# 128 unused bytes in SBUF, and two families of tiles 4128 instead of 4096 bytes apart

## The chip, the cores and the metric

The kernel runs on one core of one Trainium2 chip. The metric is the device time of one execution in microseconds. Three runs of the kernel before took 797.56, 796.80 and 796.42 us: a median of 796.8 us.

## The reference

Two layers of a decoder trunk run over one sequence of 256 tokens with 1024 features each, all in float32:

```
for l in range(2):
    h = rms_norm(x, attn_norm[l])
    x = x + hybrid_mixer(h, ...)     # three token mixers side by side: MLA, MoBA, retention
    h = rms_norm(x, mlp_norm[l])
    x = x + square(relu(h @ w_mlp_up[l])) @ w_mlp_down[l]      # 1024 -> 4096 -> 1024
return rms_norm(x, final_norm)

def hybrid_mixer(h, w_in, ...):
    p = h @ w_in                                               # 1024 -> 6560
    o_mla, o_moba, o_ret = ...                                 # three attentions over slices of p
    merged = (sigmoid(g_mla) * (o_mla @ w_branch_mla)
              + sigmoid(g_moba) * (o_moba @ w_branch_moba)
              + sigmoid(g_ret) * (o_ret @ w_branch_ret))
    return merged @ w_out
```

Nearly all arithmetic is in the weight products: 1024 to 6560, three of 512 to 1024, 1024 to 1024, 1024 to 4096 and back.

## The kernel before, in words

**Products in three parts.** Each float32 matrix is cut into a high part (float32r, the format that TensorE streams) and the low rest, and each product is made of three matmuls: high by high, high by low, low by high. The helper `three` (lines 301 to 304) writes them: line 302 is high times `whi`, line 303 high times `wlo`, line 304 the low part times `whi`. In most of them the activations are the stationary operand, a block of 128 by 128 that TensorE loads ahead of the matmul, and the weights are the moving operand, 512 columns that stream through it.

**Weights.** They come in tiles of 128 partitions by 1024 elements (4096 bytes per partition) from one DRAM tensor, in the order in which they are used. `high_low` (lines 268 to 282) casts each into `whi` on ScalarE (line 274) and takes the rest `wlo` on VectorE (line 276). These tiles lie in a pool of their own, which the change does not touch.

**Activations.** The pool `sb` holds the rest. In it a *tag* is a ring of equally large buffers, each of the size of the largest tile that uses the tag, one behind the other in SBUF; the order of the tags is that of their first use. Two rings matter here:

- `t4`, nine buffers: the normed inputs `xs0` to `xs3` (each holds high and low part of two blocks of 128 features), the attention outputs `omlah`, `omlal`, `omobah`, `omobal`, `oreth`, `oretl`, the turned low-rank inputs `cTh`, `cTl`, the squared relus `relu` before they are turned, and some raw weights at the start (`raw0`).
- `w4k`, seven buffers: the turned relus `hidden`, high and low part in a tile each, the gates `th`, and other results of 1024 elements.

Behind them lie the ring of small tiles, the scratch tiles of the rope (`ropea`, `ropeb`), and then `Q`, `KK`, `blocks`, `prob` and `turned`. Some operands of matmuls borrow buffers there: `sums` (combinations of normed inputs for the seven-product scheme of the first MLP product) lies in those of `KK` and `prob`, and `mT` (the merged mixers, the moving operand of the output product at line 1099) in those of `Q` and `KK`.

**Order.** The program is written unit by unit (`prog`, `run`), and a scheduler orders the instructions within what the dependences allow; some stretches of TensorE are written out by hand. Waits are semaphores between the engines; transfers are issued by SyncE.

Of the kernel before, what the change touches and what calls it, by code (L numbers as in the profile page):

```python
# [7 lines left out]
F32 = mybir.dt.float32  # L8
# [5 lines left out]
P = 128  # L14
# [177 lines left out]
def trunk(ctx: ExitStack, tc: tile.TileContext, gx, wts, consts, gfin, gnorm, xtok, out):  # L192
# [7 lines left out]
    sb = ctx.enter_context(tc.tile_pool(name="sb", bufs=1))  # L200
# [20 lines left out]
    nc.gpsimd.memset(sq_cols, 0.0)  # L221
    nc.gpsimd.memset(sq_in, 0.0)
    krx = [cp.tile([P, P], F32, name=f"krx{t}") for t in range(NT)]
    for t in range(NT):
        nc.gpsimd.memset(krx[t], 0.0)

# [10 lines left out]
    started, high_first, middle = {}, [], []  # L237

    def transfer(key, raw, queue=nc.sync, parts=1):
        offset, n, c = where[key]  # L240
        sz = n * c
        for cs in (slice(0, sz),) if parts == 1 else (slice(0, 416), slice(416, sz)):
            queue.dma_start(
                raw[:, cs],
                bass.AP(tensor=wts.tensor, offset=wts.offset + offset + cs.start, ap=[[sz, P], [1, cs.stop - cs.start]]),
            )
# [42 lines left out]
        return sb.tile([P, 512], F32, name=name, tag="w2k", bufs=W2K)  # L289

    def w4k(name, dtype=F32):
        return sb.tile([P, 1024], dtype, name=name, tag="w4k", bufs=W4K)

    def two(name):
        both = w4k(name)
        return [both[:, :512], both[:, 512:]]
# [4 lines left out]
    def three(o, ah, al, bh, bl, start, stop, shared=False):  # L301
        nc.tensor.matmul(o, ah, bh, start=start, stop=False, skip_group_check=shared)  # L302
        nc.tensor.matmul(o, ah, bl, start=False, stop=False, skip_group_check=shared)  # L303
        nc.tensor.matmul(o, al, bh, start=False, stop=stop, skip_group_check=shared)  # L304
# [154 lines left out]
    def rope(xv, c0, s0, t, n, h, w=None):  # L459

        w = w or n
        cos = K[:, c0 + t * w : c0 + t * w + n][:, None, None, :].to_broadcast([P, h, 2, n])
        sin = K[:, s0 + t * w : s0 + t * w + n][:, None, None, :].to_broadcast([P, h, 2, n])
        a = sb.tile([P, 256], F32, name="ropea", bufs=1)
        b = sb.tile([P, 256], F32, name="ropeb", bufs=1)
        av = a[:, : 2 * h * n].rearrange("p (h two n) -> p h two n", h=h, two=2)
        bv = b[:, : 2 * h * n].rearrange("p (h two n) -> p h two n", h=h, two=2)
        nc.vector.tensor_mul(av, xv, cos)
        nc.vector.tensor_mul(bv, xv, sin)
        nc.vector.tensor_sub(xv[:, :, 0, :], av[:, :, 0, :], bv[:, :, 1, :])  # L470
        nc.vector.tensor_add(xv[:, :, 1, :], av[:, :, 1, :], bv[:, :, 0, :])
# [154 lines left out]

    def begin(key, tag=None, bufs=None, queue=nc.sync, parts=1):
        if tag:
            started[key] = sb.tile([P, 512 if tag == "w2k" else 1024], F32, name="raw0", tag=tag, bufs=bufs)
        else:  # L630
            started[key] = wp.tile([P, 1024], F32, name="raw", bufs=RAW)
        transfer(key, started[key], queue, parts)

    nc.sync.dma_start(GX[:, : G_END + S], gx[:, : G_END + S])
    begin((0, "b0", 0), "w2k", W2K, nc.scalar)
    begin((0, "mq", 0), "w2k", W2K)
    nc.scalar.dma_start(X[0][:, 1, :], x[:, 1, :])
    xn = Normed(G_ATT)
    xrows = [x for _ in range(NT) for x in two("xrow")]
    begin((0, "b0mq", 1), "t4", T4, parts=2)  # L640
    nc.sync.dma_start(X[0][:, 2:4, :], x[:, 2:4, :])
    begin((0, "b0mq", 2), "t4", T4)
# [14 lines left out]
    one = nc.const_aps.tensor(1.0, [P, 1], mybir.dt.bfloat16)  # L657
    for i in range(WARM):
        nc.tensor.matmul(pw, one.to_broadcast([P, P]), one.to_broadcast([P, 512]), start=True, stop=True)
# [17 lines left out]
    def layer(l, xn, before):  # L677
# [6 lines left out]
        def c_norms():  # L684
            accs = b0
            if l:
                for n in range(KD):
                    xn.square(n)
                xn.stats()
            c0.extend(two("c0"))  # L690
            for t, ct in enumerate(c0):
                nc.scalar.activation(ct[:, :416], accs[t][:, :416], AF.Copy, scale=xn.col[t])
                m = small("ssc")
                junk = sb.tile([P, S], F32, name="junk", tag="xsq", bufs=2)
                nc.scalar.activation(junk, ct[:, 0:MLA_QR], AF.Square, accum_out=m[:, 0:1])
                nc.scalar.activation(junk[:, :MLA_KVR], ct[:, MLA_QR : MLA_QR + MLA_KVR], AF.Square, accum_out=m[:, 1:2])
                nc.vector.tensor_scalar(m[:, 2:3], m[:, 0:1], 1.0 / MLA_QR, EPS, op0=ALU.mult, op1=ALU.add)
                nc.vector.tensor_scalar(m[:, 3:4], m[:, 1:2], 1.0 / MLA_KVR, EPS, op0=ALU.mult, op1=ALU.add)
                nc.gpsimd.tensor_tensor(m[:, 4:6], m[:, 2:4], neghalf[:, 0:2], op=ALU.pow)
                nc.vector.tensor_scalar(ct[:, 0:MLA_QR], ct[:, 0:MLA_QR], m[:, 4:5], None, op0=ALU.mult)  # L700
                kv = ct[:, MLA_QR : MLA_QR + MLA_KVR]
                nc.vector.tensor_scalar(kv, kv, m[:, 5:6], None, op0=ALU.mult)
                kr = ct[:, 384:416].rearrange("p (h two n) -> p h two n", h=1, two=2)
                rope(kr, K_COS_MLA, K_SIN_MLA, t, 16, 1, 32)
                for i in range(2):
                    dst = krx[t][:, 64 * (1 - i) : 64 * (1 - i) + 64].rearrange("p (two n) -> p two n", two=2)
                    nc.vector.tensor_copy(dst[:, :, 16 * i : 16 * i + 16], kr[:, 0, :, :])
# [100 lines left out]
        def qrope():  # L808
            wh, wl = load_w(l, "qrope", 0)
            qr = mla["qr"] = halves(w2k("qr"))  # L810
            for t in range(NT):
                acc = misc_tile()
                sl = slice(P * t, P * t + P)
                for k in range(2):
                    three(acc[:, :S], c["h"][:, k, sl], c["l"][:, k, sl], wh[:, k, :], wl[:, k, :], k == 0, k == 1)
                nc.scalar.activation(qr[:, t, :], acc[:, :S], AF.Copy)
                rope(qr[:, t, :].rearrange("p (h two n) -> p h two n", h=4, two=2), K_COS_MLA, K_SIN_MLA, t, 32, 4)
# [334 lines left out]
        def prepare(kind, i):  # L1152

            def load(c):
                return [load_w(l, "up", 4 * i + c + j) for j in range(2)]

            def parts(raw):
                return [high_low((l, "up", i), x, 2, 1024) for x in raw]

            b = blocks.setdefault(i, {})  # L1160
            if kind == "up":
                return load_w(l, "up", i)
            if kind == "down":
                return load_w(l, "down", i, 0)
            if kind == "m1":
                b["a"], b["c"] = load(4), load(0)
            elif kind in ("n3", "m2"):
                b[kind] = load(2 if kind == "n3" else 6)
            w = parts(b[{"n3": "n3", "m2": "m2", "n7": "c"}.get(kind, "a")])
            if kind == "m1":  # L1170
                add_tiles(b["a"], b["c"])
            elif kind == "n3":
                add_tiles(b["c"], b["n3"])
                add_tiles(b["a"], b["n3"])
            elif kind == "m2":
                add_tiles(b["a"], b["m2"])
            return w
# [81 lines left out]
        def down(w, t, half, f):  # L1259

            cs, (hi, lo) = slice(512 * half, 512 * half + 512), hidden[f][t]
            three(accs[2 * t + half], hi, lo, w[0][:, 0, cs], w[1][:, 0, cs], f == 0, f == NF - 1)
# [44 lines left out]
        for event, i, kind, j in mlp_events(l):  # L1307
            if event == "prepare":
                prepared[i] = prepare(kind, j)
                continue  # L1310
            if i == len(units) - ENDS:
                break
# [38 lines left out]
        if last:  # L1351
            gf = sb.tile([P, 2, D], F32, name="gf", tag="KK", bufs=1)
            nc.sync.dma_start(gf[:, 0, :], bass.AP(tensor=gfin.tensor, offset=gfin.offset, ap=[[0, P], [1, D]]))
        ws = [prepared.pop(i) if i in prepared else prepare(*units[i]) for i in range(len(units) - ENDS, len(units))]
        order_pe = ExitStack()
        order_pe.enter_context(tc.manual_schedule(engines={mybir.EngineType.PE}))

        def finish(q, fs):
            for i in fs:
                down(ws[i], *quarters[q], NF - ENDS + i)  # L1360

# [50 lines left out]
        for t in range(NT):  # L1412
# [12 lines left out]
            else:  # L1425

                more = misc_tile("plast")
                for half, o in enumerate((accs[3], more)):
                    cs = slice(512 + 256 * half, 768 + 256 * half)
                    for i, w in enumerate(ws):  # L1430
                        three(
                            o[:, 0:256], *hidden[NF - ENDS + i][1], w[0][:, 0, cs], w[1][:, 0, cs],
                            half == 1 and i == 0, i == ENDS - 1,
                        )
# [40 lines left out]
W4K = 7  # L1475
# [7 lines left out]
XIN = (36, 39, 42, 45)  # L1483
XSQ = (44, 46, 49, 50, 53)
WARM = 8
ENDS = 4
FIRST = 4
AHEAD = 1
# [79 lines left out]
```

## Time and profile before

| What | Value |
|---|---|
| Median of three runs | 796.8 us |
| The profiled execution: its time | 797.22 us |
| Its span, from the first to the last instruction | 795.3 us |
| TensorE matmuls: busy | 788.0 us (99% of the span), 3780 records |
| VectorE busy | 671.6 us (84%) |
| ScalarE busy | 527.6 us (66%) |
| Mean granted TensorE clock | 0.999 |
| Matmuls on the chain that ended last | 98% of the span |

How to read it: a matmul's duration in the trace goes from its start to the last of its results, and the next one starts before that. So durations of neighbouring matmuls overlap, and what one costs in a row is the time from its start to the next start. Groups are named by line, engine, operation, and output <- inputs; the last numbers of a group are its busy time, the mean duration of one in ns, and the idle time of the engine before them.

### The profile page before, as it was taken

The numbers are of one execution on the slowest core, as the hardware profiler recorded it, in microseconds if no ns is written. First come the engines' busy times: TensorE is split into PE (matmuls) and PEld (weight loads), VectorE is DVE, ScalarE is ACT, GpSimd is POOL, SyncE is SP. The second block draws the span as 40 slices with busy tenths as digits, with TensorE's granted clock in tenths as the row PEclk, the third lists the DMA queues.
The fourth block names the chain that finished last, engine by engine and source line by source line (L and its number), as shares of the span: only waits on it lengthen the run. The fifth ranks groups of instructions, "written<-read, shape, count | busy, mean of one in ns | idle before, by whom it ended". The sixth has DMA issues, their size and how long they took to land.

```text
span 795.3 us, 11143 instructions
## 1 busy us (share of the span) xinstructions
PE 788.0 (99%) x3780; PEld 654.0 (82%) x3780; DVE 671.6 (84%) x1121; ACT 527.6 (66%) x821; POOL 22.0 (3%) x36
## 2 busy tenths in 40 slices
PE   9999999999999999999999999999999999999996
PEld 7888878888888888888888888788888888888885
DVE  6887897687799999998589578968878999999984
ACT  7786656544577877777586767546455778676772
POOL 0100000100000000003100000001000000000000
PEclk9999999999999999999999999999999999999999
DMA  9895989587564997667567678895975559888771
GB/s 351 306 323 187 297 271 296 204 269 247 172 238 133 278 303 255 222 198 253 190 209 250 219 229 266 296 308 175 297 248 169 191 164 324 268 283 254 256 239 54
DMA packets 76105, 192.76 MB, mean 242 GB/s; under 512 B 8576, under 2 KB 32784, under 8 KB 76048
## 3 DMA queue, kind: packets, MB, share of 16 engines
q1 hardware_dynamic: 75312, 191.20, 73.6%
q10 hardware_dynamic: 576, 0.83, 0.3%
q8 instruction: 30, 0.49, 0.2%
q14 instruction: 27, 0.22, 0.1%
q0 software_dynamic: 160, 0.02, 0.0%
HBM read 169.97 MB, written 22.04 MB: 241 GB/s over the span
## 4 chain that ended last, share of the span: by engine, by line
PE 98%; DVE 1%; DMA 0%; ACT 0%; issue 0%; POOL 0%; POOLq 0%
PE acc L302 23%; PE acc L304 22%; PE acc L303 22%; PE acc L1099 6%; PE pup L303 5%; PE pup L302 5%; PE pup L304 5%; PE po L577 1%; PE ps_s L863 1%; PE ps_s L545 1%; PE misc L303 1%; PE misc L304 1%; PE misc L302 1%; PE acc L751 0%; PE acc L754 0%; PE acc L752 0%
## 5 line engine op out<-in xcount | busy, mean ns | idle before, releaser
L274 ACT ACTIVATE whi<-raw 128x1024 fp32r<-128x1024 f32 (+3 forms) x261 | 263.9, 1026 | 145.5 <-PE acc L304 77.5
L276 DVE TENSOR_TENSOR wlo<-raw,whi 128x1024 fp32r<-128x1024 f32 (+3 forms) x262 | 303.3, 1173 | 48.7 <-ACT whi L274 48.1
L302 PE MATMUL acc<-whi,xs 128*128 128x512 f32 (+1 forms) x448 | 175.1, 394 | 0.0
L303 PE MATMUL acc<-wlo,xs 128*128 128x512 f32 (+1 forms) x448 | 174.4, 389 | 0.0
L304 PE MATMUL acc<-whi,xs 128*128 128x512 f32 (+1 forms) x448 | 173.9, 389 | 0.0
L302 PEld LDWEIGHTS acc<-whi,xs 128*128 128x128 f32 x448 | 84.1, 188 | 18.0 <-issue 1.7
L304 PEld LDWEIGHTS acc<-whi,xs 128*128 128x128 f32 x448 | 84.1, 188 | 17.1
L303 PEld LDWEIGHTS acc<-wlo,xs 128*128 128x128 f32 x448 | 84.2, 188 | 16.6
L303 PE MATMUL acc<-wlo,hidden 128*128 128x512 f32 (+1 forms) x256 | 97.1, 388 | 0.0
L304 PE MATMUL acc<-whi,hidden 128*128 128x512 f32 (+1 forms) x256 | 93.7, 389 | 0.0
L302 PE MATMUL acc<-whi,hidden 128*128 128x512 f32 (+1 forms) x256 | 83.9, 389 | 0.0
L274 ACT ACTIVATE whi<-rawlong 128x1024 fp32r<-128x1024 f32 x60 | 62.7, 1055 | 17.3 <-DVE rawlong L1181 8.7
L276 DVE TENSOR_TENSOR wlo<-rawlong,whi 128x1024 fp32r<-128x1024 f32 x60 | 71.9, 1218 | 1.7 <-ACT whi L274 1.6
L304 PEld LDWEIGHTS acc<-whi,hidden 128*128 128x128 f32 x256 | 48.1, 188 | 10.5 <-DVE hidden L322 0.4
L303 PEld LDWEIGHTS acc<-wlo,hidden 128*128 128x128 f32 x256 | 48.1, 188 | 10.1
L302 PEld LDWEIGHTS acc<-whi,hidden 128*128 128x128 f32 x256 | 48.1, 188 | 9.9
L1181 DVE TENSOR_TENSOR rawlong<-rawlong,raw 128x1024 f32<-128x1024 f32 x36 | 43.5, 1211 | 1.2 <-DMA raw<-wts 1.2
L529 ACT ACTIVATE prob<-prob,smx 128x128 f32<-128x128 f32 x64 | 28.3, 443 | 15.8 <-DVE smx L525 15.8
L303 PE MATMUL pup<-wlo,sums 128*128 128x512 f32 x96 | 38.0, 396 | 0.0
L304 PE MATMUL pup<-whi,sums 128*128 128x512 f32 x96 | 37.9, 395 | 0.0
L302 PE MATMUL pup<-whi,sums 128*128 128x512 f32 x96 | 37.3, 395 | 0.0
L1099 PE MATMUL acc<-mT,whi 128*128 128x512 f32 x128 | 33.6, 396 | 0.0
(279 smaller groups left out, 1156.2 us busy)
## 6 DMA issues: line engine op xcount, KB each, us to landing
raw<-wts SPq DMA_DIRECT2D x240, 512.0 KB, 4.9
blocks<-far SPq DMA_DIRECT2D x104, 128.0 KB, 3.8
rawlong<-wts SPq DMA_DIRECT2D x24, 512.0 KB, 5.8
far<-relu SPq DMA_DIRECT2D x16, 512.0 KB, 4.6
far<-blocks SPq DMA_DIRECT2D x16, 384.0 KB, 4.1
turned<-far SPq DMA_DIRECT2D x64, 96.0 KB, 3.5
raw<-wts SPq DMA_DIRECT2D x6, 464.0 KB, 7.6
raw<-wts SPq DMA_DIRECT2D x4, 416.0 KB, 5.6
```

The lines of the kernel that those rows point to most:

```text
L274: nc.scalar.activation(hi[:, cs], raw[:, cs], AF.Copy)
L276: nc.vector.tensor_sub(lo[:, cs], raw[:, cs], hi[:, cs].bitcast(F32))
L302: nc.tensor.matmul(o, ah, bh, start=start, stop=False, skip_group_check=shared)
L303: nc.tensor.matmul(o, ah, bl, start=False, stop=False, skip_group_check=shared)
L304: nc.tensor.matmul(o, al, bh, start=False, stop=stop, skip_group_check=shared)
L529: nc.scalar.activation(p[:, j, a:b], p[:, j, a:b], AF.Exp, bias=m[:, 4 + c : 5 + c], scale=scale, accum_out=m[:, 8 + c : 9 + c])
L545: nc.tensor.matmul(o, a[rows], b[rows], start=True, stop=True)
L577: nc.tensor.matmul(dst, vh, moving, start=i == 0, stop=i == 1)
L863: nc.tensor.matmul(o[:, P : 3 * P], q[:, P:S], k, start=True, stop=True)
L1099: nc.tensor.matmul(o, w_k, m, start=wide and k == 0, stop=(k, wide) == jobs[-1] and k == KD - 1)
L1181: nc.vector.tensor_add(x, x, y)
```

## The change

Two numbers in the allocation of SBUF change, and no instruction is added or removed. Each engine of the two built programs has the same instructions in the same order, operand for operand except for the addresses.

1. `w4k` allocates 1024 + STEP elements, STEP being 8, and hands out the first 1024. So the seven buffers are 4128 bytes apart in place of 4096. The same is done to the raw weights that `begin` puts into the ring `t4` at the start, and since they are now the largest tiles of that ring, its nine buffers are 4128 bytes apart too.
2. The first call of `rope` allocates a tile `pad` of 32 elements (128 bytes) that nothing reads or writes.

The buffers then start at these bytes modulo 256, as the two programs place them (the built address of each, modulo 256):

| Tiles | Before | Changed |
|---|---|---|
| `whi`, `wlo`, `raw` (weights) | 128 | 128 |
| ring `t4` (nine buffers, in order) | 128, all | 128, 160, 192, 224, 0, 32, 64, 96, 128 |
| ring `w4k` (seven buffers, in order) | 128, all | 160, 192, 224, 0, 32, 64, 96 |
| of these, `hidden` | 128 | all seven of `w4k` |
| `sums`, `mT`, `Q`, `KK`, `prob`, `turned`, `blocks` | 0 | 128 |
| `K`, `x1` / `GX` | 32 / 128 | 32 / 128 |

Within a tile the blocks that matmuls read begin at multiples of 512 bytes, so a tile's place is that of its blocks. The one exception is the combined weight tiles of the first layer's start and of `b0` in the second (416 columns and what follows them, 1664 bytes further on), whose second part begins at 0 modulo 256.

```diff
@@ trunk
     krx = [cp.tile([P, P], F32, name=f"krx{t}") for t in range(NT)]
+    l_pad = [32]
@@ w4k
-        return sb.tile([P, 1024], dtype, name=name, tag="w4k", bufs=W4K)
+        return sb.tile([P, 1024 + STEP], dtype, name=name, tag="w4k", bufs=W4K)[:, :1024]
@@ rope
+        if l_pad:
+            sb.tile([P, l_pad.pop()], F32, name="pad", bufs=1)
         a = sb.tile([P, 256], F32, name="ropea", bufs=1)
@@ begin
-            started[key] = sb.tile([P, 512 if tag == "w2k" else 1024], F32, name="raw0", tag=tag, bufs=bufs)
+            started[key] = sb.tile([P, 512 if tag == "w2k" else 1024 + STEP], F32, name="raw0", tag=tag, bufs=bufs)
@@ constants
+STEP = 8
```

## The prediction

> **What bounds the kernel now.** First the page of the profile: its head, the clock row of the 40 slices, and the chain that ended last by engine.
>
> ```profile
> span 795.3 us, 11143 instructions
> PE 788.0 (99%) x3780; PEld 654.0 (82%) x3780; DVE 671.6 (84%) x1121; ACT 527.6 (66%) x821; POOL 22.0 (3%) x36
> ...
> PEclk9999999999999999999999999999999999999999
> ...
> PE 98%; DVE 1%; DMA 0%; ACT 0%; issue 0%; POOL 0%; POOLq 0%
> ```
>
> TensorE's matmuls hold 98% of the chain at the full clock. So the time is the number of matmuls times the interval between their starts, and an edit that adds or removes nothing can act only through that interval. Next, the groups by line, matmuls of 512 columns, sorted here by where the operands lie. The last number but one is the mean duration in ns.
>
> ```profile
> L302 PE MATMUL acc<-whi,xs 128*128 128x512 f32 (+1 forms) x448 | 175.1, 394 | 0.0
> L303 PE MATMUL acc<-wlo,xs 128*128 128x512 f32 (+1 forms) x448 | 174.4, 389 | 0.0
> L304 PE MATMUL acc<-whi,xs 128*128 128x512 f32 (+1 forms) x448 | 173.9, 389 | 0.0
> L303 PE MATMUL acc<-wlo,hidden 128*128 128x512 f32 (+1 forms) x256 | 97.1, 388 | 0.0
> L303 PE MATMUL pup<-wlo,xs 128*128 128x512 f32 x72 | 28.0, 389 | 0.0
> ...
> L303 PE MATMUL pup<-wlo,sums 128*128 128x512 f32 x96 | 38.0, 396 | 0.0
> L1099 PE MATMUL acc<-mT,whi 128*128 128x512 f32 x128 | 33.6, 396 | 0.0
> ...
> L751 PE MATMUL acc<-whi,xs 128*128 128x512 f32 x16 | 6.4, 398 | 0.0
> L752 PE MATMUL acc<-whi,xs 128*128 128x512 f32 x16 | 6.3, 392 | 0.0
> L754 PE MATMUL acc<-wlo,xs 128*128 128x512 f32 x16 | 5.0, 395 | 0.0
> ```
>
> The upper five have stationary and moving operand at the same place, 128 modulo 256: 388 to 389 ns (394 where waits are in the mean). The lower five have them 128 bytes apart: `sums` is stationary at 0 while the weights stream from 128; `mT` streams from 0 past weights at 128; at lines 751 to 754 it is the weight tile's second part that streams from 0, in 14 of each 16. They take 392 to 398. `pup<-wlo,xs` and `pup<-wlo,sums` are the same line in the same stage, with the same moving tiles: there, only the stationary tile differs.
>
> Is a longer duration a longer interval? The timeline of TensorE (start, duration, instruction):
>
> ```profile
> 242.14 0.39 PE L302 MATMUL pup<-whi,xs 128*128 128x512 f32 x1
> ...
> 247.35 0.40 PE L304 MATMUL acc<-whi,xs 128*128 128x512 f32 x1
> ...
> 253.59 0.39 PE L303 MATMUL pup<-wlo,sums 128*128 128x512 f32 x1
> ...
> 255.91 0.39 PE L304 MATMUL pup<-whi,sums 128*128 128x512 f32 x1
> ```
>
> From the first to the second row are 23 intervals: 5.21 / 23 = 0.2265 us. From the third to the fourth are 10: 2.32 / 10 = 0.232 us. So 5.5 ns of the 7 show in the interval; I take 6 ns for a pair 128 bytes apart, the difference of the medians below.
>
> **The change part by part.** *The 128 unused bytes* bring `sums` and `mT` from 0 to 128, to the place of the weights. Duration min/median/max by tile:
>
> ```profile
> L304 PE MATMUL pup<-whi,sums x96: 390/395/404, 248.5 to 745.9; 128*128 128x512 f32 x96
> L1099 PE MATMUL acc<-mT,whi x128: 387/393/477, 205.2 to 620.4; 128*128 128x512 f32 x128
> L1099 PE MATMUL acc<-mT,wlo x128: 274/281/287, 206.2 to 621.5; 128*128 128x256 f32 x128
> L302 PE MATMUL acc<-whi,hidden x256: 278/389/478, 261.5 to 787.1; 128*128 128x512 f32 x126, 128*128 128x256 f32 x2
> L304 PE MATMUL plast<-whi,hidden x4: 279/283/283, 787.7 to 788.8; 128*128 128x256 f32 x4
> ```
>
> `sums`: 288 matmuls by 395 - 389 = 6 ns are 1.7 us less. `mT` at 512 columns: 128 by 393 - 389 = 4 ns are 0.5 us less. At 256 columns the sign turns: parted 281, together 283 (`plast`), so 128 by 2 ns are 0.25 us more. Together -2.0 us. `Q` and `KK` move together and keep their distance of 0. `prob`, `blocks` and `turned` move by 128 as well; of these only `prob` and `turned` meet TensorE, in float32 products:
>
> ```profile
> L862 PE MATMUL ps_s<-KK,Q 128*128 128x128 f32 x32 | 6.2, 274 | 0.0
> L975 PE MATMUL por<-rv,prob 128*128 128x128 f32 x16 | 3.1, 275 | 0.0
> L1040 PE MATMUL pmt<-K,th 128*128 128x128 f32 x16 | 2.4, 272 | 0.0
> ```
>
> Together (line 862) they take 274, parted by 128 (975) 275: nothing for the few there are. Line 1040 streams `K` from place 32 past `th` at 128 in 272 ns: a start at an odd 32 bytes costs nothing by itself there.
>
> *The 4128 bytes* part what was together. Counted in the changed program, 2306 float32r matmuls of 512 columns lose the common place (1290 of `xs`, 756 of `hidden`, 256 of the attention outputs, 4 of `cTh`): 440 get 128 bytes apart, 778 are 96 away on either side, 522 are 64 away, 566 are 32 away. Some 270 of `xs` and outputs stay together. The trace prices only the 440: 6 ns each, 2.6 us. For the others the ends are these. Dearest that a row shows: any parting costs as much as 128 bytes, 2306 by 6 ns = 13.8 us. In proportion to the distance: (440 + 3/4 of 778 + 1/2 of 522 + 1/4 of 566) by 6 ns = 1426 by 6 = 8.6 us. Nothing for them: 2.6 us in all. Below nothing: the 256-column row has parted pairs 2 ns *faster*, which on 2306 would be 4.6 us of gain. I take the middle of the first two, 11.2 us. My reason is that together the interval repeats at 0.2265 us, while the parted durations scatter from 390 to 404 around 395: it looks as if a common place keeps loading and streaming in step, and any other lets them drift, whatever the distance. That is argued from one distance.
>
> Against this stands a page. The Trainium skill, "TensorE: Matmul & The Clock Gate", section "Step-by-step: what each phase is for", has TensorE read the streaming operand and the weights to be loaded through two independent SBUF ports, so that loading does not steal from streaming. By that rule places could not matter; the 389 and 396 of one line in one stage speak against it. The time it gives is among the rivals.
>
> *Writers and transfers.* VectorE and ScalarE write into the shifted tiles. VectorE's rows (by form) already show two places, the inputs in `GX` at 24 modulo 32 and `x` at a multiple of 32:
>
> ```profile
> L318 DVE SCALAR_TENSOR_TENSOR xs<-GX,xs 128x256 fp32r<-128x256 f32 x12 | 5.7, 477 | 0.0
> L318 DVE SCALAR_TENSOR_TENSOR xs<-x,GX,xs 128x256 fp32r<-128x256 f32 x12 | 5.6, 477 | 3.1 <-ACT xs L317 3.1
> ```
>
> 477 both: nothing. Transfers out of `relu` and into the first `raw0` start at other places too. They hide behind TensorE's queue of work: 0% of the chain is DMA. If that cover went, one late `relu` (4.6 us from issue to landing) would show:
>
> ```profile
> far<-relu SPq DMA_DIRECT2D x16, 512.0 KB, 4.6
> ```
>
> *Waits that give way.* Line 302's mean of 394 against 389 is 448 by 5 ns = 2.2 us in which TensorE waited for weights; slower matmuls give these time. Between 0 and 2.2 us, I take 0.8.
>
> *Sum*, against the profiled execution's 797.2 us: -2.0 + 11.2 - 0.8 = +8.4 us, so 805.6. The profiled one lies 0.4 over the median of 796.8, so the forecast is 805.2.
>
> **The rivals.**
> - *Half places.* Only the half of each 256 bytes counts: 160, 192 and 224 are as good as 128. Then the 1270 matmuls from 0, 32, 64 and 96 lose: 7.6 - 2.8 = +4.8, 801.6 us. For it: both known places are ends of halves. Against: nothing.
> - *Dearer places.* An odd 32 bytes costs more than 6 ns: with the 9 ns of line 751 (398) on all 2306, 20.8 - 2.8 = +18, about 814.8. Against: the 272 of line 1040. With 8 ns it is 812.4.
> - *Only 128 apart costs*, the nearer distances nothing: 2.6 - 2.0 = +0.6, 797.4 us, no change to be measured (0.2%, 1.6 us, is what this kernel's measurement can tell).
> - *Places don't matter*, by the page's rule above or because the 6 ns belong to how `sums` and `mT` are laid out: 796.8. Against: the lines 751 to 754, where `xs` itself takes 392 to 398 with weights from 0.
> - *Parted is better* (the other side). The next weights load under the running stream where the places differ, as in the 256-column row (281 against 283): -4.6 - 2.0, 790.2 us. It decides if the wide ones at 32 to 96 bytes behave as the narrow do. Against: every parted 512-column row is slower.
> - *Only the gains come*: the near distances cost nothing and 128 apart costs nothing in `xs` and `hidden`: -2.0, 794.8.
>
> **How the numbers follow.** Forecast, proportional to full price for each parting, 802.6 to 807.8 us (8.6 and 13.8, less 2.8): 0.52. Half places 0.10, dearer 0.09. So slower 0.71. Only 128 apart 0.07 and no matter 0.05: same 0.12. Parted better 0.09, only the gains 0.08: faster 0.17. The range from 795 to 811.5 leaves out parted better, the dearer cases and the lower part of only the gains, a little under 2 in 10.
>
> **What would show it.** In the groups by line, `pup<-wlo,sums` should fall from 396 to 389 and `acc<-mT,whi` from 396 to about 392: the first step. `acc<-wlo,hidden` should rise from 388 to 392 to 395, `acc<-wlo,xs` to about 393, with TensorE still near 98% of the chain. If `hidden` rises and the time does not, waits took it. If `hidden`, which has no buffer left at 128, stays at 388, my reading of the places is wrong. If it falls, parted is better. A rise only in the buffers at 0 would be the half of it that the trace had shown.

## The result

The changed kernel takes 808.6 us (median of four runs, 808.45 to 809.20) against 796.9 us before: a ratio of 1.0145, 95% interval 1.0132 to 1.0157, some 11.7 us slower. The span of the profiled execution grows by 12.1 us, from 795.3 to 807.4. The profiled executions of e5 and e12 below ran at a granted clock of 0.75 and 0.81 (985.8 and 912.7 us); they are left out of the medians, and no rows of them are shown.

From the page and the groups by line of the changed kernel (lines 224 and following have moved down by one, those from the rope's scratch tiles on by three, those from line 1486 on by four):

```profile
span 807.4 us, 11143 instructions
PE 799.6 (99%) x3780; PEld 654.0 (81%) x3780; DVE 672.5 (83%) x1121; ACT 528.5 (65%) x821; POOL 22.0 (3%) x36
...
L303 PE MATMUL acc<-whi,xs 128*128 128x512 f32 (+1 forms) x448 | 177.2, 399 | 0.0
L304 PE MATMUL acc<-wlo,xs 128*128 128x512 f32 (+1 forms) x448 | 176.3, 394 | 0.0
L304 PE MATMUL acc<-wlo,hidden 128*128 128x512 f32 (+1 forms) x256 | 98.2, 392 | 0.0
L304 PE MATMUL pup<-wlo,sums 128*128 128x512 f32 x96 | 37.5, 391 | 0.0
L1102 PE MATMUL acc<-mT,whi 128*128 128x512 f32 x128 | 33.5, 396 | 0.0
L304 PE MATMUL pup<-wlo,xs 128*128 128x512 f32 x72 | 28.4, 394 | 0.0
```

All other engines are as busy as before within 1 us; TensorE has 11.6 us more. `xs` goes from 389 to 394 ns, `hidden` from 388 to 392 in the mean (its median goes from 389 to 394), and `sums` falls from 396 to 391. `mT` stays at 396.

Both programs have the same matmuls in the same order, so they can be paired one by one. The difference of the intervals from start to next start, added up by what is stationary (for `mT`: moving), 512 columns. Those of any width whose interval is over 245 ns in either trace stand in a row of their own, since something else than the pace sets these intervals:

| Matmuls | Number | Longer by, us |
|---|---|---|
| `xs` | 1529 | +7.25 |
| `hidden` | 750 | +3.51 |
| attention outputs | 288 | +1.73 |
| `sums` | 288 | -1.14 |
| `mT` | 124 | -0.11 |
| over 245 ns in either trace | 65 | +0.8 |
| all else | 735 | +0.05 |

That is the whole 12.1 us. And by the distance of the stationary from the moving operand, modulo 256, the mean interval in the changed kernel is:

| Bytes apart | 0 | 32 | 64 | 96 | 128 | 160 | 192 | 224 |
|---|---|---|---|---|---|---|---|---|
| ns | 229.7 | 232.5 | 232.7 | 233.2 | 232.2 | 232.8 | 232.8 | 232.8 |

In this mixture no distance but 0 is cheaper than another, and even at 0 the 229.7 is more than the 227.5 of the same distance in the kernel before.

### The profile page after: what moved, and what is told of

It reads as the page before. It is cut to its first block, busy times and chain, and to the rows that moved or that the text cites. A ratio compares the mean times of both kernels' runs of the same rounds, so it can differ in the third digit from the quotient of the medians.

```text
span 807.4 us, 11143 instructions
## 1 busy us (share of the span) xinstructions
PE 799.6 (99%) x3780; PEld 654.0 (81%) x3780; DVE 672.5 (83%) x1121; ACT 528.5 (65%) x821; POOL 22.0 (3%) x36
## 4 chain that ended last, share of the span: by engine, by line
PE 94%; ACT 2%; DMA 2%; DVE 1%; POOL 1%; issue 0%; SPq 0%; POOLq 0%; ACTq 0%
PE acc L303 22%; PE acc L305 21%; PE acc L304 21%; PE acc L1102 6%; PE pup L305 5%; PE pup L303 5%; PE pup L304 4%; PE po L580 1%; DMA blocks<-far 1%; PE ps_s L866 1%; PE ps_s L548 1%; ACT whi L275 1%; DMA far<-relu 1%; PE misc L303 1%; PE misc L304 1%; PE misc L305 1%
## 5 line engine op out<-in xcount | busy, mean ns | idle before, releaser
L303 PE MATMUL acc<-whi,xs 128*128 128x512 f32 (+1 forms) x448 | 177.2, 399 | 0.0
L304 PE MATMUL acc<-wlo,xs 128*128 128x512 f32 (+1 forms) x448 | 176.3, 394 | 0.0
L305 PE MATMUL acc<-whi,xs 128*128 128x512 f32 (+1 forms) x448 | 175.7, 393 | 0.0
L305 PE MATMUL acc<-whi,hidden 128*128 128x512 f32 (+1 forms) x256 | 94.8, 393 | 0.5 <-DVE hidden L323 0.5
L303 PE MATMUL acc<-whi,hidden 128*128 128x512 f32 (+1 forms) x256 | 85.2, 394 | 0.1
L303 PEld LDWEIGHTS acc<-whi,hidden 128*128 128x128 f32 x256 | 48.1, 188 | 11.6 <-ACT hidden L322 0.5
```

## The experiments

The theory: a float32r matmul of 512 columns repeats at 226.7 ns when its operands lie at the same place modulo 256 bytes, and at some 232 to 233 when they do not, whatever the distance. The rivals: 128 is a good place in itself; it is the changing from place to place that costs; the price goes with the distance; or `sums` and `mT` were slow for their own layout. Each experiment below changes addresses alone (e7 to e10 also the size of the scratch space for DMA descriptors); the matmuls and their order stay those of the kernel before.

### e1: the 128 unused bytes alone

```diff
-STEP = 8
+STEP = 0
```

> Only the 128 unused bytes; the buffers stay 4096 bytes apart, so every float32r matmul has stationary and moving operand at 128 modulo 256 (but for the second parts of the combined weight tiles). Theory of the common place: sums falls from 396 to 389 ns and mT from 396 to about 390, and the time by 2.0 us, to about 795 us. Rival, that the 396 belong to how sums and mT are laid out: their durations and the time stay as before.

Measured: 795.8 us, ratio to before 0.9979 (0.9969 to 0.9988), faster by 0.2% and the lowest median of this study. Groups by line:

```profile
L304 PE MATMUL acc<-wlo,xs 128*128 128x512 f32 (+1 forms) x448 | 174.3, 389 | 0.0
L304 PE MATMUL acc<-wlo,hidden 128*128 128x512 f32 (+1 forms) x256 | 96.9, 388 | 0.0
L305 PE MATMUL pup<-whi,sums 128*128 128x512 f32 x96 | 37.4, 389 | 0.0
L1102 PE MATMUL acc<-mT,whi 128*128 128x512 f32 x128 | 33.4, 395 | 0.0
```

At line 305 `sums` falls from 395 to 389 by nothing but its address, so its layout was not the reason. `mT` hardly falls (395), though it too is now at the place of the weights. The timeline suggests why: `mT` stands in fours of wide matmuls between fours of narrow ones, and what comes behind a narrow one is not at once in step, even at a common place.

```profile
618.71 1.12 PE L1102 MATMUL acc<-mT,wlo 128*128 128x256 f32 x8
619.66 0.40 PE L303 MATMUL acc<-whi,xs 128*128 128x512 f32 x1
619.89 0.40 PE L304 MATMUL acc<-wlo,xs 128*128 128x512 f32 x1
620.13 0.39 PE L305 MATMUL acc<-whi,xs 128*128 128x512 f32 x1
620.36 0.40 PE L303 MATMUL acc<-whi,xs 128*128 128x512 f32 x1
620.59 0.39 PE L304 MATMUL acc<-wlo,xs 128*128 128x512 f32 x1
620.82 0.39 PE L305 MATMUL acc<-whi,xs 128*128 128x512 f32 x1
...
624.90 0.39 PE L305 MATMUL acc<-whi,xs 128*128 128x512 f32 x1
```

The first five intervals behind the narrow ones are (620.82 - 619.66) / 5 = 0.232 us; the next 18 are (624.90 - 620.82) / 18 = 0.2267 us. Over all stretches of one common place in this trace, the mean interval is 233.0 ns for the first matmul, 230.8 for the sixth, 227.3 for the eleventh and 226.7 from the fifteenth on. So at a common place the stream falls into step, that is, it settles at a constant short interval, and that takes about ten matmuls. Why a common place does this, no run shows.

### e2: the 4128 bytes alone

```diff
-    l_pad = [32]
+    l_pad = []
```

> Only the 4128 bytes: sums and mT stay at 0, xs, hidden and the attention outputs are spread. If the two parts of the change simply add: the changed kernel's 808.6 plus the 2 us of the pad, about 810.6 us. If the spread alone sets TensorE's pace and sums and mT were already paying for what surrounds them: 808 to 809 us, as with both.

Measured: 809.4 us, ratio 1.0151 (1.0138 to 1.0164). That is just above the second expectation: beside the spread the 128 bytes are worth 0.06% (1.0151 against 1.0145), 0.5 us, which is within the intervals of both ratios, and not the 1.5 us that e1 shows. The mean interval of `sums` is 232.5 ns here, 229.1 in the changed kernel and 226.9 in e1: with spread `xs` matmuls between them, `sums` comes to its common place out of step again and again.

### e3: everything at 64

192 unused bytes ahead of the weight tiles as well, so that weights, activations, `sums` and `mT` lie at 64 modulo 256.

```diff
+    cp.tile([P, 48], F32, name="padc")
     warm = cp.tile([1, 8], F32, name="warm")
...
-STEP = 8
+STEP = 0
```

> As e1, but 192 unused bytes ahead of the weight tiles too: weights, activations, sums and mT all move to 64 modulo 256 together. Theory that only the difference of the places counts: as e1, about 795 us, 389 ns everywhere. Rival, that 128 is a good place in itself (all that lay at 0 was slow, whatever it met): every matmul at 64 pays some 6 ns, 3000 of them, about 813 us.

```profile
L304 PE MATMUL acc<-wlo,xs 128*128 128x512 f32 (+1 forms) x448 | 174.3, 389 | 0.0
L305 PE MATMUL acc<-whi,hidden 128*128 128x512 f32 (+1 forms) x256 | 93.6, 388 | 0.5 <-DVE hidden L323 0.5
L303 PE MATMUL acc<-whi,hidden 128*128 128x512 f32 (+1 forms) x256 | 84.0, 389 | 0.7 <-ACT hidden L322 0.7
L305 PE MATMUL pup<-whi,sums 128*128 128x512 f32 x96 | 37.4, 389 | 0.0
```

The durations are those of e1, so 128 is not a good place in itself: the difference decides. The time is 796.9 us, ratio 0.9990 (0.9979 to 1.0002), 1.1 us over e1 and not the 795 expected, though the two intervals overlap. TensorE's steady intervals are equal to e1's (mean 227.4 ns at distance 0 in both). The two profiled executions lie 3.0 us apart, and 2.1 us of that are long intervals: wide matmuls of over 245 ns add 7.5 us to the others' pace here, 5.4 in e1 and 4.5 before. Of this some 3.7 us in each are the 32 matmuls that follow a float32 product; the rest are waits, two of which, for `hidden`, show in the rows (e1 has one, of 0.5 us). Why these waits differ between kernels that differ in addresses alone was not tested.

### e4: one constant distance of 64 bytes

```diff
+    sb.tile([P, 16], F32, name="pad0", bufs=1)       # ahead of the first tile of the pool sb
...
-STEP = 8
+STEP = 0
```

> As e1, but 64 unused bytes ahead of the activations alone: weights at 128, all activations at 192, one constant distance of 64 bytes. Theory that any parting costs the full 6 ns: some 3000 matmuls by 6 ns less the 458 that paid before, about +15 us, 811 to 813 us, at 394 to 396 ns everywhere. Rival, that changing from place to place costs and a constant distance does not: about 795 to 797 us. Price in proportion to the distance (a half of 6 ns): about +6, 803 us.

```profile
L304 PE MATMUL acc<-wlo,xs 128*128 128x512 f32 (+1 forms) x448 | 176.7, 394 | 0.0
L304 PE MATMUL acc<-wlo,hidden 128*128 128x512 f32 (+1 forms) x256 | 98.5, 394 | 0.0
L305 PE MATMUL pup<-whi,sums 128*128 128x512 f32 x96 | 38.0, 396 | 0.0
L1103 PE MATMUL acc<-mT,wlo 128*128 128x256 f32 x128 | 18.5, 278 | 0.0
```

Measured: 811.1 us, ratio 1.0172 (1.0159 to 1.0185). One distance held throughout costs more than eight places mixed, since no matmul is left at a common place, against 696 in the changed kernel. The changing was not the cost, and 64 bytes have no discount where the stationary operand lies above the moving one (at the higher address): 2828 matmuls of 512 columns, 233.3 ns in the mean. In the other 166, `mT` and the second parts of the combined weight tiles, it lies 64 bytes below, and these take 229.8. So the direction seems to count, which the theory does not foresee; but these are also other tiles, and the two were not tested apart. The narrow matmuls of `mT` get shorter, from 282 ns in e1 to 278, and its wide ones lose nothing by being parted this way (229.9 against 230.6 ns in e1).

### e5 and e11: 256 bytes apart

e4 with a `pad0` of 64 elements in place of 16.

> As e1, with 256 unused bytes ahead of the activations: weights at 384 modulo 512, all activations at 128 modulo 512. If 256 bytes are the period, this is e1 again: 389 ns, 795 to 796 us. If the period is longer, all float32r matmuls are parted as in e4: 394 to 396 ns, about 811 us.

> The same kernel as e5, for its profile at the full clock. If 256 bytes are the period: 389 ns in the groups of xs, hidden and sums, as in e1. If not: 394 to 396 ns.

Measured: 797.2 us, ratio 0.9992 (0.9981 to 1.0003), as e3. The rows below are of e11, the same kernel (one run, 796.9 us).

```profile
L304 PE MATMUL acc<-wlo,xs 128*128 128x512 f32 (+1 forms) x448 | 174.3, 389 | 0.0
L305 PE MATMUL pup<-whi,sums 128*128 128x512 f32 x96 | 37.4, 389 | 0.0
```

389 ns: 256 bytes apart is as good as together. So 256 bytes are a period, and 32, 64 or 128 are none, as these cost in the table above, and 64 in e4.

### e6: `wlo` alone at another place

```diff
+        if w_pad:
+            wp.tile([P, w_pad.pop()], F32, name="padw", bufs=1)      # 128 bytes
         lo = wp.tile([P, 1024], F32R, name="wlo", bufs=6)
...
+    sb.tile([P, 96], F32, name="pad0", bufs=1)       # brings the activations back to 128
...
-STEP = 8
+STEP = 0
```

> As e1, but only the tiles of wlo lie at 0; whi and all activations stay at 128. One matmul in three (line 303, high times wlo) streams from another place than its stationary operand. If each matmul pays for its own pair alone: 1000 by 6 ns, +6 us on e1, about 801.5 us, with 395 ns at the line of wlo and 389 at the other two. If a parted one also throws its neighbours out of step: all three lines at 391 to 395 and +10 to +15 us, 806 to 811 us.

Measured: 803.2 us, ratio 1.0072 (1.0050 to 1.0094). `sums` by tile (duration min/median/max); lines 306, 307 and 308 are the three of `three`:

```profile
L306 PE MATMUL pup<-whi,sums x96: 389/389/398, 249.9 to 750.6; 128*128 128x512 f32 x96
L307 PE MATMUL pup<-wlo,sums x96: 387/395/398, 250.6 to 750.9; 128*128 128x512 f32 x96
L308 PE MATMUL pup<-whi,sums x96: 388/388/397, 250.8 to 751.1; 128*128 128x512 f32 x96
```

In `sums` each matmul pays for its own pair: 395 at `wlo`, 388 to 389 beside it. In the products of `xs` that make up most of the kernel, the neighbours pay too:

```profile
L306 PE MATMUL acc<-whi,xs 128*128 128x512 f32 (+1 forms) x448 | 176.6, 398 | 0.0
L307 PE MATMUL acc<-wlo,xs 128*128 128x512 f32 (+1 forms) x448 | 176.1, 393 | 0.0
L308 PE MATMUL acc<-whi,xs 128*128 128x512 f32 (+1 forms) x448 | 174.7, 391 | 0.0
```

In e1, as in the kernel before, these three lines have 394, 389 and 389. Paired with e1 (intervals up to 245 ns), the 977 parted matmuls of 512 columns take 5.6 us more and the 2011 at a common place 2.9 us more, 2.6 of these in `xs`. The time, 7.4 us over e1, lies between the 6 expected of local payment and the 10 to 15 of the other: the larger part is local, and a parted matmul also keeps some neighbours out of step.

### e7 and e8: `hidden` 4 and 16 bytes further on

```diff
-        return sb.tile([P, 1024 + STEP], dtype, name=name, tag="w4k", bufs=W4K)[:, :1024]
+        k = 1 if name == "hidden" else 0             # e8: 4
+        return sb.tile([P, 1088], dtype, name=name, tag="w4k", bufs=W4K)[:, k : k + 1024]
...
-STEP = 8
+STEP = 0
```

The scratch space for DMA descriptors is halved to make room; e9 and e10 have this too.

> As e1, but hidden alone starts 4 bytes further on (its buffers are 4352 bytes apart, so that all seven share the place 132). 756 matmuls. If any difference parts: 394 to 395 ns at hidden, +4.5 us on e1, about 800 us. If the places are counted in lines of 16 bytes or more: 389 ns, 795 to 796 us.

> As e7 with 16 bytes in place of 4. If 16 bytes part as 32 do: 394 to 395 ns at hidden, +4.5 us on e1, about 800 us. If the line is 32 bytes or more: 389 ns, 795 to 796 us.

Measured: 799.6 us, ratio 1.0029 (1.0016 to 1.0042), with 4 bytes; 796.1 us, 0.9982 (0.9972 to 0.9993), with 16. `hidden` by tile, first of e7, then of e8:

```profile
L304 PE MATMUL acc<-whi,hidden x256: 279/392/506, 261.2 to 790.0; 128*128 128x512 f32 x126, 128*128 128x256 f32 x2
```

```profile
L304 PE MATMUL acc<-whi,hidden x256: 277/389/502, 260.7 to 787.4; 128*128 128x512 f32 x126, 128*128 128x256 f32 x2
```

Four bytes cost nearly the full price, in each of the eight groups of `hidden` (231.7 to 232.5 ns in the mean). Sixteen cost little in sum, but not because each matmul pays a little. The timeline of e8 on both sides of a wait for `hidden`, which lies at the same place throughout:

```profile
376.06 0.39 PE L304 MATMUL acc<-whi,hidden 128*128 128x512 f32 x1
...
383.54 0.39 PE L304 MATMUL acc<-whi,hidden 128*128 128x512 f32 x1
...
384.57 0.50 PE L306 MATMUL acc<-whi,hidden 128*128 128x512 f32 x1 [0.42 <-DVE hidden L324]
...
385.14 0.40 PE L305 MATMUL acc<-wlo,hidden 128*128 128x512 f32 x1
...
389.35 0.39 PE L305 MATMUL acc<-wlo,hidden 128*128 128x512 f32 x1
```

Ahead of the wait 33 intervals take (383.54 - 376.06) / 33 = 0.2267 us, behind it 18 take (389.35 - 385.14) / 18 = 0.234 us. At 16 bytes the stream keeps a step that it brings along. Behind four of the five waits of this trace that broke it near `hidden`, it went on at the full price until matmuls at a common place (`sums`) restored the step or the stretch ended; behind one (at 698 us) it fell back into step by itself. So five groups lie at 226.7 to 227.0 ns and three at 230.0 to 233.4. Four bytes part (the first of e7's two expectations), and 16 part only behind a break, which neither expectation of e8 had.

One rival remains open: the second operand of the pair. In the trace of e1 the load of the next stationary block (LDWEIGHTS) starts together with the running matmul; 98% of the 3780 loads start within 6 ns of a matmul's start:

```profile
622.18 0.39 PE L305 MATMUL acc<-whi,xs 128*128 128x512 f32 x1
622.18 0.19 PEld L303 LDWEIGHTS acc<-whi,xs 128*128 128x128 f32 x1
```

So what the moving tile meets may be the next matmul's stationary block and not its own. In nearly all matmuls both are at the moving tile's place or neither is. Where they differ, the traces disagree: with its own together and the next apart a matmul takes 231.7 ns in the kernel before (38 matmuls) and 234.0 in e7 (55), the other way round 233.4 (38) and 230.3 (53). Which of the two counts stays open.

### e9 and e10: sixteen distances

As e7, with another distance for each of the eight groups of `hidden`.

> As e7, but the eight groups of hidden (96 matmuls each over both layers) lie 32, 64, 96, 128, 160, 192, 224 and 240 bytes past the place of the weights, one distance per group. If every distance parts except 16 forwards: intervals of 232 to 233 ns in all eight groups, and the time of e7, 799 to 801 us. If the place is a matter of order (the loaded block one line ahead is fine, behind is not): 240 (16 behind) at 232 too. If it is a matter of nearness: 240 at 227, and 32 and 224 between 227 and 233.

> As e9 with 8, 16, 24, 48, 80, 112, 176 and 248 bytes for the eight groups. If starts off the 16-byte line cost and whole lines do not: 8, 24 and 248 at 232 ns, 16, 48, 80, 112 and 176 at 227. If only 0 and 16 are free: 16 at 227 to 228, all others at 231 to 233.

Measured: 799.3 us each, one run, beside 797.7 of the kernel before. Mean interval of the 96 matmuls of a group (80 at 240 and 248; those over 245 ns left out), from the starts in the two traces; 0, 4 and 16 with a star are `hidden` in e1, e7 and e8:

| Bytes | 0* | 4* | 8 | 16 | 16* | 24 | 32 | 48 | 64 | 80 |
|---|---|---|---|---|---|---|---|---|---|---|
| ns | 227.0 | 232.3 | 231.1 | 229.2 | 228.3 | 230.8 | 232.6 | 232.8 | 233.2 | 231.6 |

| Bytes | 96 | 112 | 128 | 160 | 176 | 192 | 224 | 240 | 248 |
|---|---|---|---|---|---|---|---|---|---|
| ns | 233.7 | 233.0 | 232.7 | 233.0 | 230.1 | 229.0 | 233.2 | 227.8 | 233.0 |

The ends of the last two stretches in the timelines, 240 bytes in e9 and 248 in e10, start to start over seven intervals:

```profile
396.21 0.39 PE L304 MATMUL acc<-wlo,hidden 128*128 128x512 f32 x1
...
397.80 0.39 PE L305 MATMUL acc<-whi,hidden 128*128 128x512 f32 x1
```

```profile
396.22 0.40 PE L304 MATMUL acc<-wlo,hidden 128*128 128x512 f32 x1
...
397.86 0.39 PE L305 MATMUL acc<-whi,hidden 128*128 128x512 f32 x1
```

1.59 / 7 = 0.227 us sixteen bytes behind the weights, 1.64 / 7 = 0.234 us eight bytes behind. So 16 bytes behind the weights the stream runs in step at the end of its stretch, and 8 bytes behind it does not; no distance goes below 0. Neither rule that the expectations offer fits all: nearness holds for 240 but not for 4 and 248, the 16-byte line not for 48 and 112, and 192 (229.0) and 176 (230.1) stand between without a reason that these runs give. The 192 agrees with e4, where 64 bytes below took 229.8. Each distance stands in one group only, so for those between the extremes, as the 16 of e10 in a group that was out of step in e8 as well, the mean may be that of its group's breaks as much as of its distance.

### e12: only the ring of the inputs spread

The changed kernel with `w4k` unspread and 224 unused bytes ahead of it, which keep `hidden` at 128.

```diff
-        return sb.tile([P, 1024 + STEP], dtype, name=name, tag="w4k", bufs=W4K)[:, :1024]
+        return sb.tile([P, 1024], dtype, name=name, tag="w4k", bufs=W4K)
...
+    sb.tile([P, 56], F32, name="padx", bufs=1)
     xrows = [x for _ in range(NT) for x in two("xrow")]
```

> The changed kernel with hidden back at 128 (its buffers 4096 bytes apart again); only the ring of the normed inputs and attention outputs is spread. If each matmul pays for its own place and the parts add: 6 ns for 1550 matmuls on e1's 795.8, 804 to 805 us, with hidden at 389 and xs at 394 ns. If the spread throws the neighbours out of step too: hidden at 391 to 392 in the stretches where it alternates with xs, 806 to 808 us.

Measured: 806.0 us, ratio 1.0100 (1.0083 to 1.0117). The interval is 803.9 to 806.6 us and touches both expectations, so it does not decide between them; the groups by line, which would, are missing. By the ratios, it is 1.21% over e1 (9.6 us) and e7, with `hidden` alone parted by 4 bytes, is 0.50% over it (4.0 us); together 13.6 us, and the changed kernel is 1.66% over it (13.2 us). Within these intervals the two parts add.

## Why the prediction was right, and where its sum was off

The direction and the mechanism held: nothing but TensorE's intervals moved, and 808.6 lies in the range. The forecast of 805.2 was 3.4 us short. No two misses cancelled: of the 3.7 us that the forecast's +8.4 lacks of the 12.1 us of the traces, 1.3 are the discount, 0.75 the gain of the 128 bytes and 1.6 the waits, all on the same side. By its own steps:

- **What bounds the kernel.** Right. The 12.1 us of the span are intervals of matmuls.
- **The price of a pair.** Taken as 6 ns from medians; the newly parted matmuls, paired with themselves before, became 5.2 ns longer (2275 pairs without waits, 11.9 us), and in e4 the difference to e1 is 6.3 (`hidden` 233.3 against 227.0 ns). The 6 was fair, a little high for the mixture.
- **The discount for small distances: the step that failed.** "I take the middle of the first two, 11.2 us", between full price and price in proportion to the distance. There is no proportion at 32 to 128 bytes: the three groups of newly parted operands cost 7.25 + 3.51 + 1.73 = 12.5 us. Of these, 0.6 us are 261 matmuls that kept their common place and still lost 2.2 ns each; their stretches are of at most 19 matmuls and nearly all of 12 or fewer, too short to fall into step for long. The sentence given as the reason for uniform price ("any other lets them drift, whatever the distance") was the better guide than the mean that was taken of it.
- **The 128 bytes: -2.0 us.** The term of `sums` was right by itself: e1 gives (233.1 - 226.9) by 288 = 1.8 us against 1.7. Beside the spread it is 1.1. The terms of `mT` were both off: its wide matmuls gained 0.11 us beside the spread and 0.14 in e1 in place of 0.5, as wide fours between narrow fours are seldom in step, and its narrow ones lost nothing (118.5 ns before, 118.6 after) in place of 0.25.
- **Waits that give way: -0.8 us.** There was nothing to give way. Line 302's mean of 394 does not come from waits for weights: the 20 intervals of over 245 ns in its group all stand behind a float32 product, at 313 to 418 ns, and are the same in the changed kernel within 10 ns, where line 303 still has 399 beside the 394 of line 304. In the other direction, 0.9 us were added at one place: at 390 us four matmuls take 500, 332, 930 and 342 ns around waits for `hidden`, of which before only two were long (412 and 335). Why that wait grew was not tested.
- **Writers, transfers, odd 32 bytes.** Right: VectorE and ScalarE have 0.9 us more each over the whole span, and the eight places do not differ among themselves. The rival of dearer places fell.
- **The other rivals.** Half places fell (places 160, 192 and 224, distances 32 to 96, cost as much as place 0), and so did only 128 apart, only the gains, and parted is better for 512 columns; for 256 columns it holds at 64 bytes (e4: 278 ns against 282 in e1, too little to matter here) but not at 128, where `mT` takes 281 before and 283 in e6. *Places don't matter* fell with e1 and e4. The Trainium skill, "TensorE: Matmul & The Clock Gate", section "Step-by-step: what each phase is for", says that loading the next weights does not steal read bandwidth from the running matmul. No run here contradicts two ports as such, but the interval is not free of the place: 389 against 394 to 396 ns for the same instructions, and the measurement decides.

## What to carry to other kernels

Where TensorE is the bound with float32r matmuls of 512 columns, compare the addresses of stationary and moving tiles modulo 256 bytes: equal places cost nothing to arrange and were worth 2% here (e4 against e1), and an innocent unused 32 bytes between buffers takes them away. Compare the mean duration of one line's groups that differ only in a tile; 389 beside 395 ns under one line is how it shows. In this kernel a stretch of fifteen or more wide matmuls at one place ran in step, while a change of width or place, or a stall, cost some ten matmuls at the slower pace.

## What the runs showed that was not expected

- The price is mostly a matter of step and not of distance: 226.7 ns in step, and outside it a scatter with a mean of 232 to 233, be the distance 4, 32 or 128 bytes. The exceptions are a stationary operand held 64 or 80 bytes below (229.0 to 230.1).
- Falling into step takes about ten matmuls at a common place (233.0 ns for the first, 226.7 from the fifteenth on, in e1).
- 16 bytes above keep a step but mostly do not restore it (0.2267 us ahead of a wait, 0.234 behind it, in e8); 16 below restored it (227.8 ns in the mean, e9); 4 and 8 bytes do neither (232.3 and 231.1, and 233.0 at 8 behind). What reads in this pattern was not found.
- The 128 bytes' gain in TensorE's pace (some 2 us) was only in part a gain in time: by medians 1.5 us in e1, and 0.4 in e3 and 0.2 in e5 with equal matmul durations, the latter two within the noise. In the traces, long intervals take 0.9 us more than before in e1, 3.0 in e3 and 2.0 in e11.
